# Row-wise dot products and a softmax: which rows of HBM each partition loads

## The chip, the cores and the metric

The kernel runs on one core of a Trainium2 chip. The metric is device time in microseconds (us) for one launch: 325.5 us, the median of three runs (325.48 to 325.61). The core's work is done by TensorE, VectorE (DVE), ScalarE (ACT), GpSimd (POOL) and SyncE (SP); data moves between HBM and the on-chip memory through 16 DMA engines, which work off the transfers that SP and ACT put into their queues.

## What is computed

For each of 8 batches, `x` and `y` hold 4096 rows of 512 fp32 values. Only the diagonal of `x yᵀ` is used, so what is needed is one dot product for each row pair, and then a softmax over the 4096 dot products of a batch.

```python
B, N, D = 8, 4096, 512
gram = np.matmul(x, y.transpose(0, 2, 1))
diag = np.diagonal(gram, axis1=1, axis2=2)
diag = diag - diag.max(axis=-1, keepdims=True)
exp = np.exp(diag)
return (exp / exp.sum(axis=-1, keepdims=True)).astype(np.float32)
```

Each input has 8 x 4096 x 512 x 4 bytes = 67.1 MB, so 134.2 MB are read; the output has 131 KB.

## The kernel before

There are P = 128 partitions. A batch has N = 4096 rows, that is R = 32 rows for each partition, and they are loaded in two halves of H = 16 rows. The views `xv`, `yv` (L27, L28) and `ov` (L29) say which rows of HBM belong to which partition: partition p owns the 32 consecutive rows 32p to 32p+31. A half is then 16 consecutive rows (32 KB) for each partition, and the 128 runs of 32 KB lie 64 KB apart in HBM: the other half of the batch fills the spaces.

`load` takes one half of x and of y (4 MB each) into the tiles `xt` and `yt`. Both are issued on SP's queue: L43 for `xt`, L44 for `yt`. The pool `io` has three buffers for each of the two, so up to three halves are loaded or in use at a time, and SP waits before it issues the load of a half until DVE has finished with the half three before it. The last half of the last batch is loaded in pieces of 8, 4, 2, 1 and 1 rows per partition, x and y in turn, ten transfers in place of two; there the runs in HBM are 16 KB down to 2 KB long.

`dots` runs on DVE (L51): 16 instructions for each half, each multiplying one row of `xt` by the same row of `yt` on all partitions and accumulating the product's sum into one column of `diag`. Column 32b + r0 + k holds the dot product of row k of a half that begins at r0.

`softmax` follows after the second half of a batch: the maximum over the 32 columns on DVE (L65), over the partitions on GpSimd (L67), the negated maximum (L69), exp with its sum on ACT (L71), the sum over partitions on GpSimd (L76), the reciprocal (L78) and the scaling (L79) on DVE, and the store of 32 values for each partition, issued on ACT's queue (L80). `res` and `diag` have columns of their own for each batch, so no later batch waits for a store through them.

The source order is: for each batch, load and dots of half 0, load and dots of half 1, softmax.

Of the kernel before, what the change touches and what calls it, by code (L numbers as in the profile page):

```python
# [1 line left out]

# [5 lines left out]


@with_exitstack
def kernel(
    ctx: ExitStack,
    tc: tile.TileContext,
    x: bass.AP,
    y: bass.AP,
    out: bass.AP,
):
    nc = tc.nc
    f32 = mybir.dt.float32  # L20
    B, N, D = x.shape
    P = nc.NUM_PARTITIONS
    R = N // P
    H = R // 2


    xv = x.rearrange("b (p r) d -> b p r d", p=P)  # L27
    yv = y.rearrange("b (p r) d -> b p r d", p=P)  # L28
    ov = out.rearrange("b (p r) -> b p r", p=P)  # L29

    io = ctx.enter_context(tc.tile_pool(name="io", bufs=3))
    persist = ctx.enter_context(tc.tile_pool(name="persist", bufs=1))
    sm = ctx.enter_context(tc.tile_pool(name="sm", bufs=2))

    diag = persist.tile([P, B * R], f32, name="diag")
    res = persist.tile([P, B * R], f32, name="res")

    def load(b, r0, parts):
        xt = io.tile([P, H, D], f32, tag="xt", name="xt")
        yt = io.tile([P, H, D], f32, tag="yt", name="yt")  # L40
        o = 0
        for n in parts:
            nc.sync.dma_start(out=xt[:, o : o + n, :], in_=xv[b, :, r0 + o : r0 + o + n, :])  # L43
            nc.sync.dma_start(out=yt[:, o : o + n, :], in_=yv[b, :, r0 + o : r0 + o + n, :])  # L44
            o += n
        return xt, yt

    def dots(b, r0, xt, yt):
        for k in range(H):
            c = b * R + r0 + k  # L50
            nc.vector.scalar_tensor_tensor(  # L51
                out=xt[:, k, :],
                in0=xt[:, k, :],
                scalar=1.0,
                in1=yt[:, k, :],
                op0=mybir.AluOpType.mult,
                op1=mybir.AluOpType.mult,
                accum_out=diag[:, c : c + 1],
            )

    def softmax(b):
        db = diag[:, b * R : (b + 1) * R]
        rb = res[:, b * R : (b + 1) * R]
        mxp = sm.tile([P, 1], f32, tag="mxp", name="mxp")
        nc.vector.tensor_reduce(out=mxp, in_=db, axis=mybir.AxisListType.X, op=mybir.AluOpType.max)  # L65
        mx = sm.tile([P, 1], f32, tag="mx", name="mx")
        nc.gpsimd.partition_all_reduce(out_ap=mx, in_ap=mxp, channels=P, reduce_op=bass_isa.ReduceOp.max)  # L67
        nmx = sm.tile([P, 1], f32, tag="nmx", name="nmx")
        nc.vector.tensor_single_scalar(out=nmx, in_=mx, scalar=-1.0, op=mybir.AluOpType.mult)  # L69
        sump = sm.tile([P, 1], f32, tag="sump", name="sump")  # L70
        nc.scalar.activation(  # L71
            out=rb, in_=db, func=mybir.ActivationFunctionType.Exp,
            bias=nmx, scale=1.0, accum_out=sump,
        )
        ssum = sm.tile([P, 1], f32, tag="ssum", name="ssum")
        nc.gpsimd.partition_all_reduce(out_ap=ssum, in_ap=sump, channels=P, reduce_op=bass_isa.ReduceOp.add)  # L76
        rc = sm.tile([P, 1], f32, tag="rc", name="rc")
        nc.vector.reciprocal(out=rc, in_=ssum)  # L78
        nc.vector.tensor_single_scalar(out=rb, in_=rb, scalar=rc, op=mybir.AluOpType.mult)  # L79
        nc.scalar.dma_start(out=ov[b], in_=rb)  # L80

    for b in range(B):
        for h in range(2):
            last = b == B - 1 and h == 1
            parts = [8, 4, 2, 1, 1] if last else [H]
            xt, yt = load(b, h * H, parts)
            dots(b, h * H, xt, yt)
        softmax(b)


# [1 line left out]
_INS = ['x', 'y']  # L92
_OUTS = [((8, 4096), 'float32')]


# [23 lines left out]
```

## Time and profile before

| what | value |
|---|---|
| median of three runs | 325.5 us (325.48 to 325.61) |
| the profiled execution's own time | 325.61 us |
| its span (first to last recorded work) | 323.8 us |
| bytes read from HBM, rate over the span | 134.22 MB, 415 GB/s |
| L51 on DVE: 256 instructions and 256 accumulator reads | 158.3 + 21.1 us |
| DVE idle before L51, waiting for `yt` | 144.1 us in 16 waits |
| one 4 MB load, issue to landing (median) | 39.6 us for x, 48.9 us for y |
| one store, issue to landing (median; the last one) | 13.7 us; 1.4 us |

The page of a profile gives the busy time of the engines, the load of the DMA engines in 40 slices, the DMA queues (q1 takes SP's loads, q10 ACT's stores, q14 the fetching of instructions), and the chain of work that ended last. A DMA queue's "packets" are single contiguous runs plus 4-byte completion writes: q1 has 5760, which is 40 load transfers of 128 runs each and 16 completion writes for each transfer; q10 has 1152, which is 8 stores of 128 runs and 16 completion writes each. "Share of 16 engines" is the time that the packets took, divided by sixteen times the span (or the window). The time from issue to landing of a load contains its wait behind earlier loads in the same queue.

### The profile page before, as it was taken

To read this page: it belongs to the slowest core of one execution; us is meant where nothing else is said; L and a number is where in the kernel's file an instruction comes from. 1 tells how busy PE (TensorE), PEld (TensorE's weight loads), DVE (VectorE), ACT (ScalarE), POOL (GpSimd) and SP (SyncE) were. 2 spreads that over 40 slices of the span, in tenths; PEclk is the share of its full clock that TensorE was granted. 3 is DMA by queue.
4 is the path that set the end of the run, shared out by engine and by line. 5 is a ranking of instruction groups with operands and counts; after the bars stand their busy time and mean duration, and the time that the engine had idled before them with its cause. 6 is when DMAs were issued, how large, how long until landed. Compare 5 with 4: busy or idle time off the path is not lost.

```text
span 323.8 us, 727 instructions
## 1 busy us (share of the span) xinstructions
DVE 164.4 (51%) x544; ACT 4.6 (1%) x17; POOL 6.1 (2%) x20
## 2 busy tenths in 40 slices
DVE  0019075290944709256191742908348091571994
ACT  1000000000000000000000000000000000000000
POOL 0000000000000000000000000000000000000000
DMA  8999999999999999999999999999999999999980
GB/s 324 453 401 441 453 410 429 455 409 433 449 397 451 445 401 446 450 398 449 449 397 450 452 393 453 445 397 455 445 397 453 446 394 453 445 397 425 429 319 10
DMA packets 6917, 134.39 MB, mean 415 GB/s; under 512 B 1792, under 2 KB 1792, under 8 KB 2560
## 3 DMA queue, kind: packets, MB, share of 16 engines
q1 hardware_dynamic: 5760, 134.22, 96.6%
q10 hardware_dynamic: 1152, 0.13, 0.3%
q14 instruction: 5, 0.04, 0.0%
HBM read 134.22 MB, written 0.13 MB: 415 GB/s over the span
## 4 chain that ended last, share of the span: by engine, by line
DMA 82%; DVE 16%; issue 1%; SPq 0%; POOLq 0%; POOL 0%; DVEq 0%
DMA yt<-in_y_dram 82%; DVE xt L51 16%; SPq L43 0%; DVE mxp L65 0%; POOLq L114 0%; POOL mx L67 0%; DVE res L79 0%; DVE rc L78 0%; DVEq L51 0%; DVEq L79 0%; POOLq L67 0%
## 5 line engine op out<-in xcount | busy, mean ns | idle before, releaser
L51 DVE SCALAR_TENSOR_TENSOR xt<-xt,yt 128x512 f32<-128x512 f32 x256 | 158.3, 687 | 144.1 <-DMA yt<-in_y_dram 144.1
L51 DVE DVE_READ_ACCUMULATOR xt<-xt,yt 128x1 f32 x256 | 21.1, 82 | 0.0
L67 POOL PARTITION_ALL_REDUCE mx<-mxp x8 | 2.8, 350 | 308.9 <-DVE mxp L65 308.9
L71 ACT ACTIVATE res<-diag,nmx 128x32 f32<-128x32 f32 x8 | 2.6, 321 | 315.2 <-DVE nmx L69 315.2
L78 DVE RECIPROCAL rc<-ssum 128x1 f32<-128x1 f32 x8 | 1.3, 164 | 7.6 <-POOL ssum L76 7.6
L69 DVE TENSOR_SCALAR nmx<-mx 128x1 f32<-128x1 f32 x8 | 1.2, 154 | 4.3 <-POOL mx L67 4.3
L76 POOL PARTITION_ALL_REDUCE ssum<-sump x8 | 3.1, 383 | 5.8 <-ACT res L71 5.8
L79 DVE TENSOR_SCALAR res<-res,rc 128x32 f32<-128x32 f32 x8 | 1.9, 241 | 0.9
L65 DVE TENSOR_REDUCE mxp<-diag 128x1 f32<-128x32 f32 x8 | 1.5, 186 | 0.3
L71 ACT ACTIVATION_READ_ACCUMULATOR res<-diag,nmx 128x1 f32 x8 | 1.5, 186 | 0.0
L71 ACT ACT_TABLE_LOAD x1 | 1.3, 1283 | 0.7 <-PEq L103 0.7
L103 POOL MEMSET const-float32-0.0<- 128x1 f32 x1 | 0.1, 98 | 0.2 <-issue 0.2
L103 POOL MEMSET const-bfloat16-1.0<- 128x1 bf16 x1 | 0.1, 102 | 0.0
L103 POOL MEMSET const-uint8-127<- 128x1 uint8 x1 | 0.1, 101 | 0.0
L103 POOL MEMSET const-float32-1.0<- 128x1 f32 x1 | 0.1, 98 | 0.0
## 6 DMA issues: line engine op xcount, KB each, us to landing
xt<-in_x_dram SPq DMA_DIRECT2D x15, 4096.0 KB, 39.6
yt<-in_y_dram SPq DMA_DIRECT2D x15, 4096.0 KB, 48.9
xt<-in_x_dram SPq DMA_DIRECT2D x1, 2048.0 KB, 34.7
yt<-in_y_dram SPq DMA_DIRECT2D x1, 2048.0 KB, 39.3
xt<-in_x_dram SPq DMA_DIRECT2D x1, 1024.0 KB, 41.3
yt<-in_y_dram SPq DMA_DIRECT2D x1, 1024.0 KB, 43.4
xt<-in_x_dram SPq DMA_DIRECT2D x1, 512.0 KB, 35.5
yt<-in_y_dram SPq DMA_DIRECT2D x1, 512.0 KB, 27.0
```

What stands on the lines that cost most here:

```text
L51: nc.vector.scalar_tensor_tensor(out=xt[:, k, :], in0=xt[:, k, :], scalar=1.0, in1=yt[:, k, :], op0=mybir.AluOpType.mult, op1=mybir.AluOpT ...
L65: nc.vector.tensor_reduce(out=mxp, in_=db, axis=mybir.AxisListType.X, op=mybir.AluOpType.max)
L67: nc.gpsimd.partition_all_reduce(out_ap=mx, in_ap=mxp, channels=P, reduce_op=bass_isa.ReduceOp.max)
L69: nc.vector.tensor_single_scalar(out=nmx, in_=mx, scalar=-1.0, op=mybir.AluOpType.mult)
L71: nc.scalar.activation(out=rb, in_=db, func=mybir.ActivationFunctionType.Exp, bias=nmx, scale=1.0, accum_out=sump,)
L76: nc.gpsimd.partition_all_reduce(out_ap=ssum, in_ap=sump, channels=P, reduce_op=bass_isa.ReduceOp.add)
L78: nc.vector.reciprocal(out=rc, in_=ssum)
L79: nc.vector.tensor_single_scalar(out=rb, in_=rb, scalar=rc, op=mybir.AluOpType.mult)
L103: nc = _bacc.Bacc("TRN2", target_bir_lowering=False, num_devices=1)
```

## The change

The three views are cut in another order. Half h of a batch now is the 2048 consecutive rows 2048h to 2048h+2047, and partition p owns 16 consecutive rows of each half. A whole load of a half is one contiguous stretch of 4 MB in HBM: the 128 runs of 32 KB follow one another directly, 32 KB apart. The transfers keep their number, sizes, order and queue, the pieces of the last half too (their runs now lie 32 KB apart instead of 64 KB).

The 32 results of a partition, which were 128 contiguous bytes in the output, become two runs of 64 bytes, 8 KB apart; the store's view of `res` is split in the same way. Nothing else is edited: since the softmax goes over all 4096 values, it doesn't matter which partition holds which row.

```diff
-    xv = x.rearrange("b (p r) d -> b p r d", p=P)
-    yv = y.rearrange("b (p r) d -> b p r d", p=P)
-    ov = out.rearrange("b (p r) -> b p r", p=P)
+    xv = x.rearrange("b (h p r) d -> b h p r d", p=P, r=H)
+    yv = y.rearrange("b (h p r) d -> b h p r d", p=P, r=H)
+    ov = out.rearrange("b (h p r) -> b p h r", p=P, r=H)
...
-            nc.sync.dma_start(out=xt[:, o : o + n, :], in_=xv[b, :, r0 + o : r0 + o + n, :])
-            nc.sync.dma_start(out=yt[:, o : o + n, :], in_=yv[b, :, r0 + o : r0 + o + n, :])
+            nc.sync.dma_start(out=xt[:, o : o + n, :], in_=xv[b, r0 // H, :, o : o + n, :])
+            nc.sync.dma_start(out=yt[:, o : o + n, :], in_=yv[b, r0 // H, :, o : o + n, :])
...
-        nc.scalar.dma_start(out=ov[b], in_=rb)
+        nc.scalar.dma_start(out=ov[b], in_=rb.rearrange("p (h r) -> p h r", r=H))
```

## The prediction

> **What bounds the kernel now.** I read the page's busy line first, then its queues and the chain that ended last.
>
> ```profile
> span 323.8 us, 727 instructions
> DVE 164.4 (51%) x544; ACT 4.6 (1%) x17; POOL 6.1 (2%) x20
> ...
> q1 hardware_dynamic: 5760, 134.22, 96.6%
> q10 hardware_dynamic: 1152, 0.13, 0.3%
> q14 instruction: 5, 0.04, 0.0%
> ...
> DMA 82%; DVE 16%; issue 1%; SPq 0%; POOLq 0%; POOL 0%; DVEq 0%
> ```
>
> No compute engine is busy for more than 51% of the span; the load queue's packets fill 96.6% of all 16 DMA engines (columns: packets, MB, share). The chain's "DVE 16%" isn't DVE as the limit: SP issues a load when DVE frees a buffer, while other loads still wait in the queue. Whether the engines ever run dry is settled by the view by stretches (start and end, length, busy time of DVE, ACT and POOL, clock, DMA share, GB/s):
>
> ```profile
> 2.00:302.00 300.00, 147.07 (x487) 2.90 (x15) 5.13 (x14) 1.00 1.00 430
> 302.00:314.80 12.80, 12.80 (x43) 0.00 (x0) 0.00 (x0) 1.00 0.96 387
> 314.80:318.40 3.60, 3.07 (x10) 0.00 (x0) 0.00 (x0) 1.00 0.06 22
> ```
>
> From 2 to 302 us the 16 engines are busy for a share of 1.00: no idle time. The last stretch shows a share of 0.06, one sixteenth: a single engine still works, for 3.6 us. The trace's records of single packets say why. Four 8 KB instruction fetches (q14) fall into the run, at 48.1, 125.7, 186.2 and 263.7 us; each took 309 to 332 ns, and the 32 KB packet behind each took 1.79 to 1.88 us in place of 1.213. That is 4 x (0.31 + 0.64) = 3.8 us, all on one engine. So the time is the sum of the packets of this late engine, from the first packet at 2.4 us to the landing of the last piece at 318.4 us, then 0.7 us of DVE and the softmax up to the store's issue at 321.58 us.
>
> The records also give the price of a packet. Of the 3840 packets of 32 KB, 2640 took 1.211 to 1.213 us and the mean is 1.2185 us. A duration so constant (27.0 GB/s) is the pace of an engine, not that of a memory that sometimes answers late.
>
> **The change, part by part.** *The loads.* Runs, sizes, count, order and queue stay; only the distance of runs goes from 64 to 32 KB. The gain is bounded by the 1.211-1.213 us that most packets already take: each engine moves 3840 / 16 = 240 of them, so 240 x (1.2185 - 1.213) = 1.3 us if every excess vanished (0.56 us of this is the first packet of each engine, with 1.21 to 2.09 us). No row shows a 32 KB distance, so the loss is bounded by the slowest stretch: among the stretches of 5 us after the start, that at 81.5 us is slowest, with a mean of 1.2277 us; all packets so would cost 240 x 0.0092 = +2.2 us. I take 0, since over two thirds of the packets are at the floor and I see no reason for either sign: bounds -1.3 and +2.2 us.
>
> The Trainium skill (DMA: Bandwidth & Descriptors, Latency and other measured facts) has copies at a pitch between rows of 512 KiB at full rate, and only half that rate at 4 MiB; it says to "lay tiles out contiguously". Both pitches here lie below its harmful ones, and the 430 GB/s of the stretch above agrees with full rate at 64 KB; the rule too would make this part 0.
>
> *The first seven stores.* A store had 128 runs of 128 bytes, 8 for each engine; it gets 256 runs of 64 bytes, 16 for each. In the packet records small packets and 32 KB packets alternate on an engine while loads are queued. From the start of a 128-byte packet to the start of the load packet behind it are 10 ns, for a 4-byte one 6 ns; I take 8 ns for 64 bytes. The late engine then pays 7 x (16 x 8 - 8 x 10) = 336 ns, 0.34 us. From below: 0, as the bytes are the same. From above: the page's 0.3% of 323.8 us on 16 engines for 1152 packets is 13.5 ns each, and 56 more of them are 0.76 us.
>
> A rule against the change stands in the same page (Specifications): below 512 B a transfer is not at line rate, because the DMA does a read-modify-write. Before, the runs were below that already, with 13 ns in the records, far from a round trip to memory; by the rule the doubled count would double what a store costs, 56 x 13 ns = 0.73 us as an estimate with the record's duration.
>
> *The last store* is alone, nothing hides it.
>
> ```profile
> q10 hardware_dynamic: 144, 0.02, 4.7%
> ...
> out_dram<-res ACTq DMA_DIRECT2D x1, 16.0 KB, 1.4
> ```
>
> This is the DMA view of 321.5 to 323.84 us. Its 144 packets start within 0.22 us (records), the rest of the 1.4 us is fixed. Twice the runs: +0.1 us, between 0 and +0.2. ACT's issue takes 0.34 us; SP's issues take 0.33 to 0.43, so a more complex pattern may add 0 to 0.1; I take 0.05.
>
> *A wait in the tail.* SP's own waits from 268 to 324 us:
>
> ```profile
> SPq L44 <- DMA xt<-in_x_dram: 9.4, 1, 9.4
> ...
> SPq L44 <- DMA yt<-in_y_dram: 4.6, 1, 4.6
> SPq L44 <- DMA out_dram<-res: 2.7, 1, 2.7
> ```
>
> The last six pieces are each issued when the transfer eight places before it has landed. The first one-row piece of `yt` waits for batch 6's store until 301.57 us, and two more pieces are queued behind it. That store gets slower: its packets alternated with 16 KB packets of 0.61 us from 295.9 us on, so 16 in place of 8 end near 295.9 + 16 x 0.61 = 305.7 us, some 5 us later. This costs nothing, because the engines have other work: the late engine ends at 318.4, the last three pieces are 3 x 8 packets x 86 ns = 2.1 us, and from a first issue to a first packet are 1.7 us (0.72 to 2.4), so the piece may be issued as late as 318.4 - 2.1 - 1.7 = 314.6 us. The other seven stores hold up nobody: no other line of SP's waits names one but the end of the program, which waits for the last.
>
> DVE, ACT and GpSimd do the same work on the same shapes: 0.
>
> **Sum.** 0 + 0.34 + 0.1 + 0.05 = +0.5 us. On the profiled execution's 325.61 us (323.8 of span, 1.8 around it) that is 326.1; it ran 0.1 us above the median, so against the median 326.0 us.
>
> **The rivals.**
>
> *The memory answers more evenly from one stretch.* For it: 1200 of 3840 packets exceed the floor, the first of each engine most. Against it: the contents of those 1.3 us may be other things than distance (the fetches above are in them: 4 x 0.65 / 16 = 0.16 us). All of it gone: 326.0 - 1.3 = 324.7 us; that is faster as soon as 1.15 us of it goes, or 0.65 us if the stores cost nothing.
>
> *The 16 engines meet in the same part of the memory* (the other side). At a distance of 32 KB the partitions that are read at one time lie within half the stretch of addresses that they took before; if fewer parts of the memory serve it, load packets get longer. Against it: at 64 KB nothing of the kind shows, at a share of 1.00. Its place is every 32 KB packet, its price 240 times the stretch: +2.2 us at the slowest stretch's mean, with the stores 328.2 us. It decides from a mean of 1.2192 us on: 240 x 0.0007 = 0.17 us, with the stores' 0.5 past +0.65.
>
> *The tail's wait becomes the limit.* If batch 6's store is worked off against 32 KB packets throughout, it lands at 295.9 + 16 x 1.21 = 315.3 us, 0.7 after the 314.6 us up to which it is free: 326.0 + 0.7 = 326.7 us. Against it: most engines are at 16 KB packets then.
>
> *The loads are cut otherwise.* With a contiguous 4 MB source the transfers might be split into other runs than 32 KB per partition, so that the load's pace is another one. The pieces show the direction: 16 KB packets took 611 ns, two of them 1.222 us, 0.009 more than one of 32 KB, thus 240 x 0.009 = +2.2 us; longer runs at most repay as much. Packet counts would tell.
>
> **How the numbers follow.** About 0.2%, 0.65 us, is what a measurement of this kernel can tell from no change. Forecast (load packets as before, the stores' small price): 62%, own range 325.4 to 327.0 us, of it 40 points below 326.15 and 22 above. More even memory: 18%, of it 15 faster, 3 same. Collision: 11%, slower. Tail: 3%, slower. Other cut: 6%, half faster, a third slower, the rest same. Together: faster 18%, same 44%, slower 38%. The range goes from the even memory's 324.6 to 327.6 us, which leaves out the worst of the collision and of a double gain.
>
> **What would show it.** Right: q1 again 5760 packets and a share near 1.00 up to 302 us; q10 with 8 x (256 + 16) = 2176 packets and a share of 0.4 to 0.5%; stores landing after some 20 us, except the last one with about 1.5; the one-sixteenth stretch again before the last landing. Wrong: a mean of 32 KB packets off 1.2185 us by more than 3 ns, another packet count on q1, stretches with a share below 0.97 before 302 us, or the late engine's lag no longer near 3.7 us.

## The result and the profile after

The changed kernel takes 326.94 us, the median of four runs (326.56 to 327.13), beside 325.51 us for the kernel before: a ratio of 1.0042 with a 95% interval of 1.0024 to 1.0059. That is 1.4 us slower. The profiled execution took 327.13 us with a span of 325.4 us, 1.5 us more than before by either.

These are the lines of the page after that answer to those shown of before:

```profile
span 325.4 us, 727 instructions
DVE 164.4 (51%) x544; ACT 4.6 (1%) x17; POOL 6.1 (2%) x20
...
q1 hardware_dynamic: 5760, 134.22, 96.1%
q10 hardware_dynamic: 2176, 0.13, 0.5%
q14 instruction: 5, 0.04, 0.0%
...
DMA 82%; DVE 16%; issue 1%; SPq 0%; POOLq 0%; POOL 0%; DVEq 0%
```

DVE's work is the same to the tenth of a microsecond. The loads' queue has the same 5760 packets; its share is lower (96.1% in place of 96.6%) only because the span is longer. The stores have 2176 packets. The view by stretches (same columns as before) has the first row unchanged:

```profile
2.00:302.00 300.00, 146.94 (x487) 2.90 (x15) 5.16 (x14) 1.00 1.00 430
302.00:314.80 12.80, 12.80 (x43) 0.00 (x0) 0.00 (x0) 1.00 0.95 383
314.80:318.40 3.60, 3.20 (x10) 0.00 (x0) 0.00 (x0) 1.00 0.06 23
```

Sixteen engines without a gap up to 302 us at 430 GB/s, and again one engine alone between 314.8 and 318.4 us. So the load phase did not move: DVE's last dot product, released by the last piece, starts at 318.45 us before and at 318.58 us after, and the mean of the 3840 load packets of 32 KB is 1.2185 us before and 1.2176 us after (packet records). The difference stands behind it, in the lines of the store's issue (duration of the issue in ns; then the time to landing):

```profile
L80 ACTq DMA_DIRECT2D out_dram<-res x8: 378/378/415, 54.4 to 321.7; - x8
...
DMA to landing us min/median/max: 2.8/22.0/23.4
```

The seven stores under the loads take a median of 22.0 us in place of 13.7; SP now waits for some of them, and that costs nothing (the wait in the tail, below). The last one, which nothing hides, takes 2.8 us in place of 1.4: the whole loss. The next two fences are the DMA view of 321.5 to 323.8 us, before and after; the row of GB/s has 40 slices of 58 ns each.

```profile
GB/s 0 0 0 0 0 0 0 0 0 0 0 0 0 0 0 2 85 107 74 18 0 142 0 0 0 0 0 0 0 0 0 0 0 0 0 0 0 0 0 0
...
q10 hardware_dynamic: 144, 0.02, 4.8%
q14 instruction: 1, 0.01, 1.3%
...
out_dram<-res ACTq DMA_DIRECT2D x1, 16.0 KB, 1.4
```

```profile
GB/s 0 0 0 0 0 0 0 0 0 0 0 0 0 0 0 0 0 0 0 35 89 97 52 11 0 0 0 0 0 142 0 0 0 0 2 0 0 0 0 0
...
q10 hardware_dynamic: 272, 0.02, 7.8%
q14 instruction: 1, 0.01, 0.8%
...
out_dram<-res ACTq DMA_DIRECT2D x1, 16.0 KB, 2.8
```

The group of small numbers is the store, the single 142 is a fetch of 8 KB of instructions, the fifth in the run. Before, it comes right behind the store. After, the store is longer and a little later; the fetch stands behind most of it, and 0.3 us after its start there is a "2": the last packets of one engine, which were overtaken. The records of the landing, one for each engine, give the price. Fifteen engines have landed by 323.28 us, 1.57 us after the issue at 321.71 (before, all sixteen by 323.00, 1.42 us after 321.58). The sixteenth lands at 324.53 us. The 1.5 us are thus 0.13 (issue later) + 0.15 (more packets) + 1.25 (one engine's last two packets and its completion, behind the fetch). Of the 1.25 us, 0.63 are the wait of these packets (the last starts at 323.50 us, on the other engines by 322.87), and 0.62 the landing after it (1.02 us in place of 0.40). The records don't name the engine; that the fetch was on it follows from the waiting packets, which start 3 to 4 ns before the fetch's recorded end in this run and in each of the six others with a late sixteenth landing. The fetch is recorded only from 323.18 us on, 0.31 us after the other engines' last packets; why this engine stood still before that, no record says.

### The profile page after: what moved, and what is told of

It is laid out like the page before. It is cut to its first block, busy times and chain, and to the rows that moved or that the text cites. A ratio compares the mean times of both kernels' runs of the same rounds, so it can differ in the third digit from the quotient of the medians.

```text
span 325.4 us, 727 instructions
## 1 busy us (share of the span) xinstructions
DVE 164.4 (51%) x544; ACT 4.6 (1%) x17; POOL 6.1 (2%) x20
## 3 DMA queue, kind: packets, MB, share of 16 engines
q1 hardware_dynamic: 5760, 134.22, 96.1%
q10 hardware_dynamic: 2176, 0.13, 0.5%
## 4 chain that ended last, share of the span: by engine, by line
DMA 82%; DVE 16%; issue 1%; SPq 0%; POOLq 0%; POOL 0%; DVEq 0%
DMA yt<-in_y_dram 82%; DVE xt L51 15%; SPq L43 0%; DVE mxp L65 0%; POOLq L114 0%; POOL mx L67 0%; DVE res L79 0%; DVE rc L78 0%; DVEq L51 0%; DVEq L79 0%; POOLq L67 0%
```

## The experiments

All times are medians; the kernel before ran beside each group (325.59 to 325.64 us). "Landing" is the time of the last store from its issue to its landing. The diffs are shortened: prefixes such as `mybir.AluOpType.` are left out.

| run | median us | ratio to before, 95% interval | landing us | fifth fetch starts at us |
|---|---|---|---|---|
| changed kernel | 326.94 | 1.0042 [1.0024, 1.0059] | 2.8 | 323.18 |
| e1 new loads, old store | 325.64 | 0.9998 [0.9990, 1.0007] | 1.4 | 322.79 |
| e2 old loads, new store | 326.72 | 1.0033 [1.0021, 1.0045] | 2.6 | 323.08 |
| e3 last store from SP | 326.76 | 1.0037 [1.0024, 1.0049] | 2.5 | 322.77 |
| e4 ACT busy behind it | 326.84 | 1.0037 [1.0024, 1.0050] | 2.5 | 322.83 |
| e5 DVE busy behind it | 326.53 | 1.0025 [1.0015, 1.0035] | 2.4 | 322.37 |
| e6 negations on ACT | 326.53 | 1.0026 [1.0017, 1.0035] | 1.6 | 326.02 |
| e7 runs of 32 bytes | 326.64 | 1.0031 [1.0020, 1.0043] | 2.6 | 322.60 |
| e8 few DVE instructions, new layout | 322.93 | 0.9918 [0.9904, 0.9931] | 1.6 | none |
| e9 few DVE instructions, old layout | 322.85 | 0.9926 [0.9912, 0.9940] | 1.4 | none |
| e10 before, DVE busy behind it | 326.79 | 1.0034 [1.0021, 1.0047] | 2.5 | 322.61 |

### Loads or store: e1 and e2

```diff
 e1, against the changed kernel
-    ov = out.rearrange("b (h p r) -> b p h r", p=P, r=H)
+    ov = out.rearrange("b (p r) -> b p r", p=P)
...
-        nc.scalar.dma_start(out=ov[b], in_=rb.rearrange("p (h r) -> p h r", r=H))
+        nc.scalar.dma_start(out=ov[b], in_=rb)
 e2, the reverse of both against the kernel before
```

> The changed loads with the store of before (one run of 128 bytes per partition); the results of a batch come out in another order. My theory: the profile after shows that 15 of 16 engines finish the last store as before and one lands 1.24 us later, because an 8 KB instruction fetch got in front of its last packets; the loads give only 0.13 us. Then this is 325.6 us (325.4 to 325.8), the last store lands 1.4 us after its issue, and the fetch stands behind the store's packets. Rival, the loads cost it: 326.9 us.

> The loads of before with the changed store (two runs of 64 bytes per partition); the results of a batch come out in another order. My theory: 326.5 to 327.1 us, the last store lands 2.5 to 2.9 us after its issue. Rival, the loads cost it: 325.5 to 325.8 us. The seven earlier stores should cost at most 0.35 us together, seen as a later landing of the last piece.

The loads alone: 325.64 us, no change. The store alone: 326.72 us, the loss of the whole change within the intervals. In e1's tail the store is again the short group, and the fetch again follows it:

```profile
GB/s 0 0 0 0 0 0 0 0 0 0 0 0 0 0 0 0 0 71 112 80 23 0 142 0 0 0 0 0 0 0 0 0 0 0 0 0 0 0 0 0
...
out_dram<-res ACTq DMA_DIRECT2D x1, 16.0 KB, 1.4
```

The rival, that the loads cost it, falls, and so do both of the prediction's rivals about the memory. What e2 should have shown of the seven earlier stores it does not show clearly: DVE's last scaling starts at 321.63 us in e2, 321.31 in the kernel before, 321.44 in the changed kernel. That is one profile of each, and kernels with equal loads and stores scatter by nearly as much: the changed kernel and its variants e3 to e6 have it between 321.16 and 321.44 us.

### Whose fetch is it: e3, e4, e5, e6

```diff
 e3
+        eng = nc.sync if b == B - 1 else nc.scalar
-        nc.scalar.dma_start(out=ov[b], ...)
+        eng.dma_start(out=ov[b], ...)
 e4, behind the store of the last batch
+            idle = sm.tile([P, 1024], f32, tag="idle", name="idle")
+            nc.scalar.activation(out=idle, in_=rb[:, 0:1].to_broadcast([P, 1024]), func=Exp)
 e5, at the same place
+            idle = sm.tile([P, 1], f32, tag="idle", name="idle")
+            nc.vector.tensor_reduce(out=idle, in_=rb[:, 0:1].to_broadcast([P, 1024]), axis=X, op=max)
 e6
-        nc.vector.tensor_single_scalar(out=nmx, in_=mx, scalar=-1.0, op=mult)
+        nc.scalar.activation(out=nmx, in_=mx, func=Copy, scale=-1.0)
```

> The changed kernel with only the last store issued from SP, which waits for its landing before it goes on to the end of the program, in place of ACT, which goes on at once. My theory, with the fetch as ACT's own step to the code that ends the program: no fetch meets the packets, landing 1.5 to 1.7 us after issue, 325.6 to 326.0 us. Rival, runs of 64 bytes are slow to land by themselves: still 2.5 to 2.9 us and 326.6 to 327.1 us. If the fetch is another engine's it stays at 326.6 to 327.1 too, but with the fetch among the store's packets.

> The changed kernel with one more instruction on ACT behind the last store (exp over 128x1024 into a tile that nobody reads), about 1 us long, so that ACT comes to its end of the program later. My theory: the fetch moves about 1 us later, behind the store's packets, landing 1.5 to 1.7 us after issue; 325.6 to 326.2 us, although there is more work. Rival, slow 64-byte runs: 326.6 to 327.1 us or more, landing as late as in the changed kernel.

My first theory had the fetch as ACT's. It fell twice: with the store on SP's queue, and with ACT busy for 1.05 us longer, the fetch still started 1.2 us after the end of DVE's last scaling (322.77 and 322.83 us), and the store still landed 2.5 us after its issue.

> The changed kernel with one more DVE instruction behind the last scaling (a maximum over 128x1024 that nobody reads, about 1.1 us), so that DVE reaches the end of its program later. With ACT busy and with SP issuing, the fetch stayed where it was, about 1.2 us after DVE's last instruction, and the four fetches before it come at DVE's pace; so I now take it for DVE's. Theory D1, the fetch belongs to DVE's step to the end of the program: it moves 1.1 us later, behind the store's packets; the last store lands 1.5 to 1.7 us after its issue (2.8 in the changed kernel); the time may gain less than 1.1 us of that, as DVE itself ends later. Theory D2, the fetch comes whenever DVE has worked off 128 instructions more: it stays among the store's packets, landing 2.5 to 2.8 us. Rival, 64-byte runs are slow by themselves: landing 2.5 to 2.8 us, with the fetch elsewhere.

> The changed kernel with the eight negations of the maximum on ACT in place of DVE: eight DVE instructions fewer (16 with waits at most). Theory D2: each of DVE's fetches comes later by a few per cent of a batch, and the fifth, which was some 1.2 us behind DVE's last instruction, does not come before the end of the store: landing 1.5 to 1.7 us, 325.6 to 326.0 us. Theory D1: the fetch stays 1.2 us behind DVE's last instruction, landing 2.5 to 2.8 us, 326.6 to 327.1 us. Rival, slow 64-byte runs: landing 2.5 to 2.8 us wherever the fetch is.

In e5 DVE was busy until 322.77 us, but the fetch came earlier, at 322.37 us: it doesn't wait for DVE to reach the end, one more instruction to be fetched draws it forward. The store landed after 2.4 us, just under what D2 expected. In e6 eight DVE instructions less put it off until 326.0 us, outside the span (in which the page now counts four fetches). Both speak against D1 and, for the fifth fetch, for D2: DVE's instructions are fetched ahead, and the fetch depends on how many of them DVE has used up. It isn't a strict count: before the five fetches of the changed kernel DVE's records number 53, 193, 306, 444 and 575, in e6 53, 191, 331, 438 and 570. Of the first four, which D2 expected all to come somewhat later, three came 0.4 us earlier in e6 and one 18 us later (203.4 in place of 185.6 us). In e6's tail the store stands alone, with its 272 packets at once:

```profile
GB/s 0 0 0 0 0 0 0 0 0 0 0 0 0 0 27 80 106 58 15 0 0 0 0 0 0 0 0 0 0 0 0 0 0 0 0 0 0 0 0 0
...
q10 hardware_dynamic: 272, 0.02, 7.8%
...
out_dram<-res ACTq DMA_DIRECT2D x1, 16.0 KB, 1.6
```

It lands after 1.6 us, so runs of 64 bytes are not slow by themselves: with twice the packets, 0.15 us more than the 1.42 of before. Yet e6 kept most of the loss, 0.9 us, and here D2's expected time (325.6 to 326.0) was wrong. Its profiled execution took 326.35 us with a span of only 323.8: 2.5 us lie around the span, in the other runs 1.8. So of the 1.25 us by which the store landed sooner after its issue, 0.75 came back outside the span, where the fetch now was. That the fetch caused this is argued from its time alone; no run separates it.

### The number of runs, or the event: e7

```diff
-    ov = out.rearrange("b (h p r) -> b p h r", p=P, r=H)
+    ov = out.rearrange("b (g p r) -> b p g r", p=P, r=8)
...
-        nc.scalar.dma_start(out=ov[b], in_=rb.rearrange("p (h r) -> p h r", r=H))
+        nc.scalar.dma_start(out=ov[b], in_=rb.rearrange("p (g r) -> p g r", r=8))
```

> The changed kernel with the store cut into four runs of 32 bytes per partition (32 packets for each engine and store); the results of a batch come out in another order. My theory, one engine is overtaken by the fetch once: the last store's landing grows by 0.1 to 0.4 us over the changed kernel's 2.5 to 2.8, and the seven earlier stores cost 16 x 7 x 7 ns = at most 0.8 us more; 327.0 to 328.2 us. Rival, the cost goes with the number of small runs: doubling again adds 1.1 to 1.4 us to the last landing (3.8 to 4.2 us), 328.0 to 328.6 us.

Doubled again, the runs cost nothing more: landing 2.6 us, 326.64 us in all, below my own theory's 327.0 to 328.2 too. The earlier stores land after 39.5 us (median); SP waits for them seven times, 142 us in all, and the engines stay full all the same (share 1.00 from 2 to 302 us). Fifteen engines land by 323.18 us, 1.78 us after the issue, and the sixteenth at 324.02. The price is that of an event, not of a count.

### The kernel before, made to meet the fetch: e10

The edit of e5, in the kernel before; its loads and its store are untouched.

> The kernel before, store and loads untouched, with one more DVE instruction behind the last scaling (a maximum over 128x1024 that nobody reads). In the changed kernel this extra instruction drew the fetch forward, to 0.8 us after the last scaling. My theory: here it draws the fetch from just behind the store's packets (0.08 us behind the last of them) into them, so that the kernel before pays what the changed one pays: the last store lands 2.1 to 2.5 us after issue instead of 1.4, and 326.1 to 326.6 us. Rival, only runs of 64 bytes land late: 1.4 us, 325.5 to 325.8 us.

```profile
GB/s 0 0 0 0 0 0 0 0 0 0 0 0 0 0 47 103 85 32 2 142 0 0 0 0 7 11 0 0 0 0 0 0 0 0 0 0 0 0 0 0
...
q14 instruction: 1, 0.01, 0.8%
...
out_dram<-res ACTq DMA_DIRECT2D x1, 16.0 KB, 2.5
```

The fetch is recorded from 322.61 us on, as long after the last scaling as before (1.16 and 1.18 us), but it ends 0.2 us sooner after it (1.46 in place of 1.67). All eight data packets of one engine stand behind it: "7 11", 0.3 us after its start. Fifteen engines land by 322.91 us, the sixteenth at 323.96. The landing takes 2.5 us and the kernel before loses 1.2 us, somewhat more than expected, without any change of layout. The added instruction by itself isn't the price: the same edit lengthened nothing in e5. So the loss doesn't need the 64-byte runs: it needs a fetch that arrives before the store's last packet.

### The late engine: e8 and e9

```diff
     def dots(b, r0, xt, yt):
+        if b < B - 1:
+            nc.vector.tensor_tensor(out=xt, in0=xt, in1=yt, op=mult)
+            nc.vector.tensor_reduce(out=diag[:, b * R + r0 : b * R + r0 + H], in_=xt, axis=X, op=add)
+            return
         for k in range(H):
```

> The changed kernel with one multiplication over 128x8192 and one sum per row in place of 16 dot-product instructions, in the first 14 of 16 halves: DVE executes about 30 + 64 + 40 instructions in place of 552 and works longer, some 17 us a half, still less than the 19.4 us of a load. If the late engine of the prediction is late by DVE's fetches, one or none of the four is left, the late engine ends 2.8 to 3.7 us earlier, the fifth fetch is gone too and the last store lands after 1.5 to 1.7 us: 326.9 - 2.8 to 3.7 - 1.1 = 322.1 to 323.0 us. Rival, the engine is late for another reason: 325.6 to 326.9 us. If DVE can't keep up, it is over 328 us.

> The kernel before (64 KB distance, runs of 128 bytes in the store) with one multiplication over 128x8192 and one sum per row in the first 14 of 16 halves. In the changed kernel this edit gave 322.93 us with one of DVE's four fetches left. My theory, the layout of the loads is worth nothing and, with no fetch near the last store, the store's runs only cost the 0.1 to 0.3 us of their own packets: 322.6 to 322.9 us, last landing 1.4 us after issue. Rival, the contiguous loads do help once the late engine is less late: 323.2 us or more.

Both beat the kernel before by 0.7 to 0.8%. The page of e8:

```profile
span 321.2 us, 312 instructions
DVE 268.5 (84%) x124; ACT 4.6 (1%) x17; POOL 6.1 (2%) x20
...
q14 instruction: 1, 0.01, 0.0%
```

DVE is busy for 268.5 us in place of 164.4, and the kernel is 2.7 us faster than the one before, since DVE's 51% had left room: DVE executes 124 instructions in place of 544, and one fetch is left of five. The stretches of e8:

```profile
2.00:302.00 300.00, 254.01 (x75) 2.90 (x14) 5.13 (x14) 1.00 1.00 431
302.00:311.00 9.00, 9.00 (x31) 0.00 (x0) 0.00 (x0) 1.00 0.99 409
311.00:314.00 3.00, 3.00 (x11) 0.00 (x0) 0.00 (x0) 1.00 1.02 380
314.00:315.60 1.60, 1.06 (x4) 0.00 (x0) 0.00 (x0) 1.00 0.07 27
```

The row with one engine alone (share 0.07) lasts only to 315.1 us, where the last load packet ends; in the changed kernel that is at 318.0 us (packet records). The 3.0 us are near the 3 x 0.95 = 2.85 us of three fetches less. e9 with the old layout takes 322.85 us, e8 with the new one 322.93 us, with intervals that overlap: with no fetch near the last store, neither the distance of the loads nor the runs of the store can be told apart from nothing.

## Why the prediction was right or wrong

*What bounds the kernel* was right: the loads' packets on 16 full engines, and at the end one engine that is late by its four instruction fetches. e8 took three of them away and got back what they had cost. The times of day that the prediction read from the packet records were 0.7 us too late, having been counted from another zero (the fetches start at 47.4, 125.0, 185.5 and 263.0 us of the span). The lengths of packets and fetches don't depend on it, but three figures of the tail do; they are set right below.

*The loads, 0 between -1.3 and +2.2 us,* was right: e1 measured a ratio of 0.9998, at most 0.1% either way.

*The first seven stores, +0.34 us* was too high. The 64-byte packets took 11 ns where 128-byte ones took 13, and on one engine followed each other in 7 ns (records of the last store). 7 x (16 x 7 - 8 x 10) = 0.22 us is left, and even that doesn't show: the loads ended 0.13 us later after the change, and with twice the packets again, in e7, they ended earlier (last scaling at 321.12 us).

*The last store, +0.1 us between 0 and +0.2,* is the step that failed. (The 0.05 us for ACT's longer issue were right: 378 ns in place of 338.) It landed 2.8 us after its issue, not the 1.5 us that the prediction named as a sign, and the sentence "the rest of the 1.4 us is fixed" was true of the fifteen engines that landed 0.15 us later than before, relative to the issue. It left out who else used the engines: the page of before had five fetches on q14, the prediction used four, and the fifth began 0.08 us behind the store's last packet (322.72 against 322.64 us). Counted from the end of the last scaling, that fetch came at 1.18 us; the old store's last packet started at 1.10, and the new store's at 1.19 on the fifteen engines that weren't held up: 0.1 us more was enough to meet it. Put in its place, the term is 0.15 + 1.25 = 1.4 us. The rule of the Trainium skill about runs below 512 B (DMA: Bandwidth & Descriptors, Specifications: not at line rate, because of a read-modify-write), which the prediction weighed for the first seven stores as a doubled packet cost of 0.73 us, didn't show as such a cost: e7 has twice the packets of the changed kernel again, of half the size, and isn't slower.

*The wait in the tail, 0,* was right. These are SP's waits from 268 us on in the changed kernel:

```profile
SPq L44 <- DMA xt<-in_x_dram: 9.4, 1, 9.4
...
SPq L44 <- DMA out_dram<-res: 7.0, 1, 7.0
...
SPq L43 <- DMA out_dram<-res: 5.5, 1, 5.5
```

The one-row piece of `yt` waits 7.0 us for batch 6's store in place of 2.7 and is issued at 306.00 us, where the prediction had 305.7 and allowed up to 314.6. Counted from the span's zero, its working gives 305.0 (that store's packets start at 295.2 us, not 295.9) and up to 315.3 (from issue to first packet are 1.0 us, not 1.7), and the rival of this wait loses its price: 295.2 + 16 x 1.21 = 314.6 us is still in time. The 5.5 us in the last line are a wait of the pieces of 4 rows for the store of batch 5, at 275.13 us; the prediction had the other seven stores hold up nobody. SP has six such waits in the whole run, 25.8 us in all, and none for a store in L43 before. They cost nothing for the same reason: the engines stay full (share 1.00 up to 302 us).

*The rivals.* More even memory and collision both fell with e1; the loads were cut as before (5760 packets). The tail's wait stayed hidden. None of them had the cause.

The time of 326.94 us lies inside the range, 0.9 us above the forecast's 326.0, yet slower than 326.15, a case that had got 38%; no change had got 44%. That the range holds the number is luck: it was made for other causes, and no part of it for a fetch in the last store's way.

## What to carry to other kernels

A transfer that nothing hides ends with the slowest of its 16 engines, so look in that window for every queue, the instruction fetches among them, and ask what stands just behind it: a step that gets 0.1 us longer, as here, can pay for what it runs into, not for its own length. When a kernel is bound by full DMA engines, the instructions of an engine that is busy for half the time may not be free, since the fetches (q14) are work of the same DMA engines: fewer, longer DVE instructions gained 2.7 us here while DVE's busy time rose by 104 us. The distance of 32 KB runs, 32 or 64 KB, made no difference that could be measured.

## What the runs showed of the hardware

The record of an 8 KB instruction fetch is 0.31 to 0.61 us long. Under the loads each delayed one engine by about 0.95 us (0.31 us and a 32 KB packet of 1.8 to 1.9 us in place of 1.21 behind it); with three fetches less the last load packet ended 3.0 us earlier (e8). A store that a fetch overtakes on one engine landed there 0.8 to 1.25 us behind the other fifteen engines (e2, e3, e4, e5, e7, e10 and the changed kernel). On that engine the landing came 0.9 to 1.0 us after the end of the fetch; on the others it came 0.36 to 0.50 us after the last completion packet (322.87 to 323.28 us in the changed kernel).

The Trainium skill (DMA: Bandwidth & Descriptors, Queues, rings and completion order) says that a completion increment lands only after every earlier write of that DMA engine, across its queues. The late landing agrees, if the fetch's own write must land first: the packets' wait alone makes 0.63 of the 1.25 us in the changed kernel. Another reason for the other 0.62 us is not excluded by any run. Before, where the fetch came behind the store's last packet, all sixteen engines landed before the fetch had ended (323.00 and 323.21 us).

The fetches come ahead of use, about one for 113 to 140 recorded DVE instructions after the first in the changed kernel. One more DVE instruction let the fifth one end 1.46 us after the last scaling (e5, e10) in place of 1.64 to 1.80 (all others with it in the span); eight fewer moved it out of the span (e6).
